# A hybrid retention and S5 layer on one core: dummy products on ones, the sample's state as moving operand, scores a slot later, a GLU operand in two pieces

## The chip, the cores and the metric

The kernel runs on one core of one Trainium2 chip. The metric is the device time of one execution in microseconds; a difference in it counts as measurable here from about 0.2% on.

## What is computed

One layer (DEPTH is 1) of a streaming encoder, for a prompt of 2048 frames and for 8 running streams of 16 frames (the sample), 1024 channels, in float32:

```python
hn = _rmsnorm(x, norm_g)
q, k, v, g_ret, u, g_ssm = split(hn @ w_in)            # 1024 x 3072
o, ret_s = _retention(rotary(q), rotary(k), v, ret_s0)  # 4 heads of 128
o = _rmsnorm(o, ret_norm_g) * silu(g_ret)
y, ssm_h = _s5(u, ssm_h0, ...)                          # 32 groups, complex scan
z = gelu(y)
z = z * sigmoid(z @ w_glu + b_glu) * silu(g_ssm)
out = x + concat([o, z]) @ w_out
y = _rmsnorm(out, final_norm_g)
```

In the retention each head keeps a state of 128x128; an output frame is its masked scores times the values plus its query times the state. For the sample there are 8 states a head, one for each stream.

## The kernel before, in words

The frames lie in 17 tiles of 128: tiles 0 to 15 are the prompt, tile 16 is the sample (8 streams of 16). Weights are split into two float16 parts, so a projection step is three products: hi by hi (L709), lo by hi (L710), hi by lo (L711) for the heads, L695 to L697 for `u` and the gate.

**The order.** The program is written out by hand in a list of slots, `stream`. A slot holds the three products of one 128-row block of the contraction (in the `u` and gate stages for one block of output columns, in the heads for one tile), and everything else hangs on a slot as a hook (`hook(i, f)` runs f right behind slot i). Each engine takes its instructions in the order of this list, and SP, which issues nearly all DMAs, too. First comes the `u` projection in six chunks of tiles, then head 0 with its 17 tiles (8 slots a tile; tile 16 is taken after tile 8), then the gate projection, heads 1 to 3 beside the S5 scans, the GLU (64 slots from `G0`), and last the output product.

**The start** (L320 to L334, L605 to L634). SP loads tile 0 and tile 1 of x, the first weights, tiles 2 to 8, then the small S5 inputs (`s5_loads`, L353 to L366), tiles 9 to 16 and the constants `C`. PE runs 13 dummy products on `warm`, a tile of zeros (L339), transposes tile 0 (`half`, L157, into the two `aux` banks and `tr`), runs 20 more dummies, and then computes the column sums of the squared weights (`mat`, L219, output `nps`), from which VectorE works out the scales of the first weights; with the transposes of tile 1 and the first split weights the stream can begin. `warm` is carved from the buffer named `ct`, and so is `hst`, into which `s5_loads` brings the S5 state of the sample.

**Weights of the next stage.** Head 0's eight weight tiles `raw` are loaded during the `u` stage by hooks from slot 9 on, every fourth slot (L183), squared on ScalarE from slot 46 on, every fifth (L196), and split later. Between these loads SP issues the stores of the finished `u` pieces (`flush_store`, L687, `ud`).

**A step of a head** (class Step; `n` is its first slot). `r0` at n+7 rotates q and k (VectorE L722, GpSimd L726) and evacuates v and the gate; `r1` at n+15 transposes q and k (L740) and copies them (`qkT`, L742); `r2` at n+17 multiplies them (`scps`, L746) and masks the scores (`sm`, L749, VectorE); `r3` at n+23 makes output and next state (L768 to L770), with `stats` for the norm (ScalarE L756, GpSimd L132 and L133, VectorE L759). `scps` lies in the bank `sc`, of which there is one and which the scale products `nps` and the third product of `sst` (below) use too.

**The sample's step** (tile 16, one a head). `r3s` at n+20 computes the output transposed: values as stationary and scores as moving operand (L787), then for each of the 8 streams its state as stationary operand and its 16 query columns as moving operand (L789); ScalarE copies the result (`oT`, L791) and at n+25 PE transposes it back (`ots`, L809). `states` at n+28 makes the new states in four banks (`sst`, L800).

**The GLU operand.** `Glu.split` scales z on ScalarE (L1275, hi part) and takes the rest on VectorE (L1276, 128x4x280), for tile t+2 while tile t is multiplied.

Of the kernel before, what the change touches and what calls it, by code (L numbers as in the profile page):

```python
# [10 lines left out]
F32 = mybir.dt.float32  # L11
# [4 lines left out]
AF = mybir.ActivationFunctionType  # L16
OP = mybir.AluOpType
# [45 lines left out]
def kernel(ctx: ExitStack, tc: tile.TileContext, eye, cst, rot, x_prompt, x_sample, state_ret,  # L63
# [5 lines left out]
    act = nc.scalar.activation  # L69
    V = nc.vector  # L70
    G = nc.gpsimd
    mm = nc.tensor.matmul
    tr = nc.tensor.transpose

    def dap(t, off, ap):
        return bass.AP(tensor=t.tensor, offset=t.offset + off, ap=ap)
# [4 lines left out]
    def right(name, st):  # L81
        return pool(name, st=st, side="right", reuse_waits="tile")
# [6 lines left out]
    def pbank(tag, name):  # L89
        return ps.tile([128, 512], F32, tag=tag, name=name, bufs=2 if tag in ("pj", "aux") else 1)  # L90
# [9 lines left out]
    ident = per.tile([128, 128], F32, name="ident")  # L100
# [12 lines left out]
    ones = per.tile([128, 128], F32, name="ones")  # L113
# [6 lines left out]
    alc, alz, syc, tsc, icc = ex[:, 16:20], ex[:, 20:21], ex[:, 21:22], ex[:, 22:23], ex[:, 23:24]  # L120
# [53 lines left out]
    class Ws:  # L174
# [10 lines left out]
        def split(self):  # L185
            d = self.t = self.dst()
            sc = self.group.gs[:, self.scale:self.scale + 1]
            act(d[:, 0, :], self.raw, AF.Copy, scale=sc)  # L188
            V.scalar_tensor_tensor(d[:, 1, :], self.raw, sc, d[:, 0, :], op0=OP.mult, op1=OP.subtract)  # L189
# [79 lines left out]
    tp = right("tp", ctx)  # L269
# [63 lines left out]
    warm = sa("ct", [128, 576])[:, 0:128]  # L333
    V.memset(warm, 0.0)  # L334
    pw = pbank("pj", "warm")

    def warm_up(n):
        for _ in range(n):
            mm(pw[:, 0:128], warm, warm, start=True, stop=True)  # L339
    warm_up(13)  # L340


    def idle(n):
# [267 lines left out]
    p = pbank("st", "smps")  # L611
# [8 lines left out]
    hns[0].half(0, "aux")  # L620
    gu.square(3, True)
    hns[0].half(1, "tr")
    warm_up(20)
    hns[1].stat()
    gu.square(4)
    gu.square(5, True)
# [72 lines left out]
    class Step:  # L699
# [37 lines left out]
        def r1(self):  # L737
# [3 lines left out]
            self.qkT = tp.tile([128, 2, 128], F32, name="qkT", bufs=2)  # L741
            act(self.qkT, p[:, 0:256].rearrange("p (q n) -> p q n", q=2), AF.Copy)  # L742

        def r2(self):
            p = pbank("sc", "scps")
            mm(p[:, 0:128], self.qkT[:, 1, :], self.qkT[:, 0, :], start=True, stop=True)  # L746
            self.sm = tp.tile([128, 128], F32, tag="sm", name="sm", bufs=1)
            L = 128 if self.t < 16 else 16
            V.scalar_tensor_tensor(self.sm, p[:, 0:128], float(GAM[self.h] ** -L), cmask if self.t < 16 else smask,  # L749
                                   op0=OP.mult, op1=OP.mult)  # L750
# [32 lines left out]
        def r3s(self):  # L783
            h_ = self.h
            Sb = self.Sb
            po = pbank("o", "ops")
            mm(po[:, 0:128], self.vt, self.sm, start=True, stop=False)  # L787
            for b in range(8):
                mm(po[:, 16 * b:16 * b + 16], Sb[:, b, :], self.qkT[:, 0, 16 * b:16 * b + 16], start=False, stop=b == 7)  # L789
            oT = tp.tile([128, 128], F32, tag="sm", name="oT", bufs=1)  # L790
            act(oT, po[:, 0:128], AF.Copy)  # L791
            self.oT = oT

        def states(self):
            Sb = self.Sb
# [7 lines left out]
                V.scalar_tensor_tensor(sv, sv, float(GAM[self.h] ** 16), pq[q].rearrange("p (b e) -> p b e", b=2),  # L803
                                       op0=OP.mult, op1=OP.add)
            dma(dap(rs_sample, self.h * 16384, [[128, 128], [65536, 8], [1, 128]]), Sb)

        def r3s2(self):
            po = pbank("tr", "ots")
            tr(po[:, 0:128], self.oT, ident)  # L809
            self.stats(po[:, 0:128])  # L810

        def r4(self):
            a = alc[:, self.h:self.h + 1]
# [9 lines left out]
    def hook(i, f):  # L823
        hooks.setdefault(max(int(i), 0), []).append(f)
# [64 lines left out]
    for s in seq:  # L889
        n = s.at  # L890
        hook(n + 7, s.r0)
        hook(n + 15, s.r1)
        hook(n + 17, s.r2)
        if s.t < 16:
            hook(n + 23, s.r3)
            hook(n + 28, s.r4)
            hook(n + 32, s.st)
        else:
            hook(n, s.r3s_load)
            hook(n + 20, s.r3s)  # L900
            hook(n + 25, s.r3s2)
            hook(n + 28, s.states)
            hook(n + 30, s.r4)
            hook(n + 33, s.st)
# [20 lines left out]
    for i in range(5):  # L925
        t, n = 4 * i, 1 if i == 4 else 4
# [5 lines left out]
    def s5(name, shape, dt=F32, bufs=1):  # L932
        return sp[0].tile(shape, dt, tag=name, name=name, bufs=bufs)
# [162 lines left out]
    for g, q in enumerate(gps):  # L1096
        n = C1 + PER * g
# [156 lines left out]
    class Glu:  # L1254
# [17 lines left out]
        def split(self):  # L1272
            z = zb[:, :, self.t, :]
            self.hl = s5("U5", [128, 4, 2, 280], F16, 2)
            act(self.hl[:, :, 0, :], z, AF.Copy, scale=syc)  # L1275
            V.scalar_tensor_tensor(self.hl[:, :, 1, :], z, syc, self.hl[:, :, 0, :], op0=OP.mult, op1=OP.subtract)  # L1276

        def mmul(self, k2):
            cb, k0 = k2 // 2, 2 * (k2 % 2)
# [28 lines left out]
    for t in range(8):  # L1308
        if t < 6:
            hook(G0 + 8 * t + 7, glus[t + 2].split)  # L1310
        n = (S5END + 3, S5END + 4, G0 + 2, G0 + 4, G0 + 22, G0 + 30, G0 + 38, G0 + 46)[t]
# [3 lines left out]
    for t in range(8):  # L1315
        for cb in range(4):
            n = G0 + 8 * t + 2 * cb + 1
# [157 lines left out]
```

## Time and profile before

| what | value |
|---|---|
| median of 3 runs | 968.43 us (967.48 to 968.7) |
| profiled execution, its own time | 965.96 us |
| its span in the trace | 964.2 us |
| VectorE, ScalarE, GpSimd busy | 66%, 45%, 35% |
| moved by DMA | 106.16 MB, mean 110 GB/s |

The span runs from the first to the last instruction of the profiled execution; its own time lies 1.8 us above. Engines are called PE (TensorE), DVE (VectorE), ACT (ScalarE), POOL (GpSimd) and SP (SyncE, the DMA issuer) in the rows; L339 is line 339 of the kernel. A product in float32 shows as two passes, so 20 products count as 40. A row of the timeline merges instructions of one line that follow each other, and the time in it runs from the first one's start to the last one's end, while products overlap: the pitch from one start to the next is shorter than the duration of one.

### The profile page before, as it was taken

What the parts mean: (1) busy time and instruction counts of PE and PEld (TensorE: products, weight loads), DVE (VectorE), ACT (ScalarE), POOL (GpSimd) and SP (SyncE); (2) the same over time, 40 slices, a digit from 0 to 9 for tenths busy, and PEclk for the clock granted to TensorE, in tenths of its full rate; (3) what the DMA queues carried; (4) which work ended last, traced back from release to release, by engine and by line L of the source; (5) the groups of instructions that cost most, each with busy time, mean ns of one, the idle gap of its engine ahead of it and who ended that gap; (6) DMA issues with size and microseconds to landing.
All of it is one profiled execution on the core that took longest, in us unless ns stands there. A gap on an engine that the chain in (4) does not pass through costs nothing.

```text
span 964.2 us, 15907 instructions
## 1 busy us (share of the span) xinstructions
PE 923.4 (96%) x5386; PEld 557.3 (58%) x5386; DVE 639.0 (66%) x1595; ACT 437.5 (45%) x1133; POOL 334.0 (35%) x620
## 2 busy tenths in 40 slices
PE   2999999999999999999999999999999999999997
PEld 2896445555687555556655566555656864444444
DVE  2569954566589756777887778887576955345344
ACT  3575323433466544545445454454434844232331
POOL 0121334432354423544565445655234420000001
PEclk7999999999999999999999999999999999999999
DMA  9696245431186435221224212374263254544542
GB/s 303 215 126 82 55 115 135 107 83 44 44 163 107 94 98 121 65 60 37 62 70 116 60 37 57 93 255 133 64 225 112 67 147 123 152 109 122 152 110 87
DMA packets 161283, 106.16 MB, mean 110 GB/s; under 512 B 80001, under 2 KB 147121, under 8 KB 160689
## 3 DMA queue, kind: packets, MB, share of 16 engines
q1 hardware_dynamic: 161056, 104.88, 42.5%
q8 instruction: 42, 0.69, 0.3%
q14 instruction: 41, 0.33, 0.1%
q10 hardware_dynamic: 144, 0.26, 0.1%
HBM read 64.69 MB, written 35.96 MB: 104 GB/s over the span
## 4 chain that ended last, share of the span: by engine, by line
PE 73%; DVE 11%; DMA 4%; ACT 4%; issue 4%; POOL 4%; SPq 0%; POOLq 0%; ACTq 0%; DVEq 0%
PE pj L709 9%; PE pj L710 9%; PE pj L711 9%; PE outps L1359 6%; PE outps L1358 6%; PE outps L1357 6%; PE ups L695 4%; PE ups L697 4%; PE ups L696 3%; PE glps L1286 2%; PE glps L1287 2%; PE glps L1288 2%; PE scps L746 1%; PE ops L770 1%; PE yps L1069 1%
## 5 line engine op out<-in xcount | busy, mean ns | idle before, releaser
L726 POOL TENSOR_TENSOR rot<-A,Pm 128x128 f32<-128x128 f32 x136 | 75.5, 574 | 120.9 <-DVE A L722 100.2
L709 PE MATMUL pj<-w,R1a 128*128 128x512 f16 x288 | 109.3, 380 | 0.0
L711 PE MATMUL pj<-w,R1a 128*128 128x512 f16 x288 | 109.1, 379 | 0.0
L710 PE MATMUL pj<-w,R1a 128*128 128x512 f16 x288 | 109.1, 379 | 0.0
L1358 PE MATMUL outps<-w,mh 128*128 128x512 f16 (+1 forms) x280 | 104.4, 373 | 0.0
L1359 PE MATMUL outps<-w,mh 128*128 128x512 f16 (+1 forms) x280 | 104.4, 373 | 0.0
L1357 PE MATMUL outps<-w,mh 128*128 128x512 f16 (+1 forms) x280 | 104.4, 373 | 0.0
L709 PE MATMUL pj<-w,R1b 128*128 128x512 f16 x256 | 97.2, 380 | 0.0
L711 PE MATMUL pj<-w,R1b 128*128 128x512 f16 x256 | 97.0, 379 | 0.0
L710 PE MATMUL pj<-w,R1b 128*128 128x512 f16 x256 | 97.0, 379 | 0.0
L729 ACT ACTIVATE vt<-pj,hv 128x128 f32<-128x128 f32 x68 | 25.0, 368 | 146.1 <-DVE A L722 144.6
L695 PE MATMUL ups<-R1a,w 128*128 128x256 f16 (+1 forms) x256 | 73.3, 286 | 2.2 <-ACT w L188 1.0
L1368 ACT ACTIVATE res<-xo 128x512 f32<-128x512 f32 (+1 forms) x35 | 21.6, 617 | 117.6 <-DVE xo L1367 69.7
L697 PE MATMUL ups<-R1a,w 128*128 128x256 f16 (+1 forms) x256 | 73.2, 286 | 0.4 <-DVE w L189 0.4
L696 PE MATMUL ups<-R1a,w 128*128 128x256 f16 (+1 forms) x256 | 73.2, 286 | 0.0
L1367 DVE SCALAR_TENSOR_TENSOR xo<-outps,ex,xo 128x512 f32<-128x512 f32 (+1 forms) x35 | 25.6, 733 | 65.2 <-PE outps L1359 65.2
L132 POOL TENSOR_TENSOR ss<-ss,C 128x1 f32<-128x1 f32 x68 | 18.8, 277 | 126.3 <-ACT sj L756 126.2
L756 ACT ACTIVATE sj<-ops 128x128 bf16<-128x128 f32 x64 | 17.7, 276 | 91.5 <-PE ops L770 91.1
L189 DVE SCALAR_TENSOR_TENSOR w<-raw,gc,w 128x512 f16<-128x512 f32 x48 | 40.8, 853 | 26.3 <-ACT w L188 26.2
L132 POOL TENSOR_TENSOR fs<-fs,half__73 128x1 f32<-128x1 f32 x16 | 3.0, 190 | 154.4 <-DVE fs L1372 154.4
L759 DVE SCALAR_TENSOR_TENSOR on<-ops,ss,gg 128x128 f32<-128x128 f32 x64 | 22.4, 350 | 47.0 <-POOL ss L133 46.7
L697 PEld LDWEIGHTS <-w 128*128 128x128 f16 x384 | 37.6, 98 | 22.1 <-DVE w L189 0.7
(352 smaller groups left out, 2373.3 us busy)
## 6 DMA issues: line engine op xcount, KB each, us to landing
raw<-in_w_in_dram SPq DMA_DIRECT2D x48, 256.0 KB
raw<-in_w_out_dram SPq DMA_DIRECT2D x32, 256.0 KB
xo<-in_x_prompt_dram SPq DMA_DIRECT2D x16, 512.0 KB
out_dram<-res SPq DMA_DIRECT2D x16, 512.0 KB
R1a<-in_x_prompt_dram SPq DMA_DIRECT2D x9, 512.0 KB
uraw<-ud SPq DMA_DIRECT2D x32, 140.5 KB
yd<-ysb SPq DMA_DIRECT2D x32, 140.0 KB
R1a<-yd SPq DMA_DIRECT2D x4, 1120.0 KB
```

The costliest lines, as they stand in the source:

```text
L189: V.scalar_tensor_tensor(d[:, 1, :], self.raw, sc, d[:, 0, :], op0=OP.mult, op1=OP.subtract)
L695: mm(ov, w[:, 0, c], hh, start=k == 0, stop=False)
L696: mm(ov, w[:, 0, c], hl, start=False, stop=False)
L697: mm(ov, w[:, 1, c], hh, start=False, stop=k == NK - 1)
L709: mm(self.pj, hh, w[:, 0, :], start=k == 0, stop=False)
L710: mm(self.pj, hh, w[:, 1, :], start=False, stop=False)
L711: mm(self.pj, hl, w[:, 0, :], start=False, stop=k == NK - 1)
L726: G.tensor_tensor(self.rot[:, :, a, :], A[:, :, a, :], Pm[:, :, 1 - a, :], OP.add if a else OP.subtract)
L1357: mm(p, m[:, k, 0, :], w[:, 0, cw], start=k == 0, stop=False)
L1358: mm(p, m[:, k, 0, :], w[:, 1, cw], start=False, stop=False)
L1359: mm(p, m[:, k, 1, :], w[:, 0, cw], start=False, stop=k == NK - 1)
L1367: V.scalar_tensor_tensor(self.x[:, c], p, icc, self.x[:, c], op0=OP.mult, op1=OP.add)
```

## The change

It does four things. The dummy products in the second batch read `ones` (L114, a tile of ones that VectorE writes at the start) instead of `warm`; the first batch is as before. In the sample's step the scores are the stationary and the values the moving operand, so the output comes out with frames on partitions; the state of a stream is now the moving operand of 128 columns and the queries are stationary, 32 columns at a time, one product for each of the four groups of 32 output partitions and for the first and second stream in it. For that `qm` holds the queries twice, with the other stream's columns zero (`r1s`: a fill on GpSimd, two copies on ScalarE, in the buffer of `Pm`). The copy `oT` and the transpose `ots` go, and `stats` follows at once; `r3s` stands at n+22 instead of n+20. `r2` stands at n+18 instead of n+17, for all tiles. `Glu.split` does its VectorE part in two pieces of 128x2x280.

```diff
--- before.py
+++ after.py
@@ -334,10 +334,10 @@
     V.memset(warm, 0.0)
     pw = pbank("pj", "warm")
 
-    def warm_up(n):
+    def warm_up(n, w):
         for _ in range(n):
-            mm(pw[:, 0:128], warm, warm, start=True, stop=True)
-    warm_up(13)
+            mm(pw[:, 0:128], w, w, start=True, stop=True)
+    warm_up(13, warm)
 
 
     def idle(n):
@@ -620,7 +620,7 @@
     hns[0].half(0, "aux")
     gu.square(3, True)
     hns[0].half(1, "tr")
-    warm_up(20)
+    warm_up(20, ones)
     hns[1].stat()
     gu.square(4)
     gu.square(5, True)
@@ -741,6 +741,13 @@
             self.qkT = tp.tile([128, 2, 128], F32, name="qkT", bufs=2)
             act(self.qkT, p[:, 0:256].rearrange("p (q n) -> p q n", q=2), AF.Copy)
 
+        def r1s(self):
+            self.qm = tp.tile([128, 2, 128], F32, tag="Pm", name="qm", bufs=1)
+            G.memset(self.qm, 0.0)
+            for a in range(2):
+                o, i = (z.rearrange("p (g b j) -> p g b j", g=4, b=2)[:, :, a, :] for z in (self.qm[:, a, :], self.qkT[:, 0, :]))
+                act(o, i, AF.Copy)
+
         def r2(self):
             p = pbank("sc", "scps")
             mm(p[:, 0:128], self.qkT[:, 1, :], self.qkT[:, 0, :], start=True, stop=True)
@@ -784,12 +791,12 @@
             h_ = self.h
             Sb = self.Sb
             po = pbank("o", "ops")
-            mm(po[:, 0:128], self.vt, self.sm, start=True, stop=False)
-            for b in range(8):
-                mm(po[:, 16 * b:16 * b + 16], Sb[:, b, :], self.qkT[:, 0, 16 * b:16 * b + 16], start=False, stop=b == 7)
-            oT = tp.tile([128, 128], F32, tag="sm", name="oT", bufs=1)
-            act(oT, po[:, 0:128], AF.Copy)
-            self.oT = oT
+            mm(po[:, 0:128], self.sm, self.vt, start=True, stop=False)
+            for b in range(2):
+                for g in range(4):
+                    r = slice(32 * g, 32 * g + 32)
+                    mm(po[r, 0:128], self.qm[:, b, r], Sb[:, 2 * g + b, :], start=False, stop=b == 1)
+            self.stats(po[:, 0:128])
 
         def states(self):
             Sb = self.Sb
@@ -803,11 +810,6 @@
                 V.scalar_tensor_tensor(sv, sv, float(GAM[self.h] ** 16), pq[q].rearrange("p (b e) -> p b e", b=2),
                                        op0=OP.mult, op1=OP.add)
             dma(dap(rs_sample, self.h * 16384, [[128, 128], [65536, 8], [1, 128]]), Sb)
-
-        def r3s2(self):
-            po = pbank("tr", "ots")
-            tr(po[:, 0:128], self.oT, ident)
-            self.stats(po[:, 0:128])
 
         def r4(self):
             a = alc[:, self.h:self.h + 1]
@@ -890,15 +892,15 @@
         n = s.at
         hook(n + 7, s.r0)
         hook(n + 15, s.r1)
-        hook(n + 17, s.r2)
+        hook(n + 18, s.r2)
         if s.t < 16:
             hook(n + 23, s.r3)
             hook(n + 28, s.r4)
             hook(n + 32, s.st)
         else:
             hook(n, s.r3s_load)
-            hook(n + 20, s.r3s)
-            hook(n + 25, s.r3s2)
+            hook(n + 16, s.r1s)
+            hook(n + 22, s.r3s)
             hook(n + 28, s.states)
             hook(n + 30, s.r4)
             hook(n + 33, s.st)
@@ -1273,7 +1275,8 @@
             z = zb[:, :, self.t, :]
             self.hl = s5("U5", [128, 4, 2, 280], F16, 2)
             act(self.hl[:, :, 0, :], z, AF.Copy, scale=syc)
-            V.scalar_tensor_tensor(self.hl[:, :, 1, :], z, syc, self.hl[:, :, 0, :], op0=OP.mult, op1=OP.subtract)
+            for c in (slice(0, 2), slice(2, 4)):
+                V.scalar_tensor_tensor(self.hl[:, c, 1, :], z[:, c], syc, self.hl[:, c, 0, :], op0=OP.mult, op1=OP.subtract)
 
         def mmul(self, k2):
             cb, k0 = k2 // 2, 2 * (k2 % 2)
```

PE at the start, before: `hnps` are the transposes of tile 0 and then tile 1, `warm` the dummies, `nps` the sums for the first scales, `ups` the `u` projection.

```order
L157 MATMUL hnps<-ident,R1a 128x128 [waits DVE_49]
L157 MATMUL hnps<-ident,R1a 128x128 x7
L339 MATMUL warm<-zf 128x128 [waits DMAHW1_49]
L339 MATMUL warm<-zf 128x128 x19
L219 MATMUL nps<-gc,ones 128x8 [waits DVE_49]
L157 MATMUL hnps<-ident,R1a 128x128 x4
L157 MATMUL hnps<-ident,R1a 128x128 [waits PE_49]
L157 MATMUL hnps<-ident,R1a 128x128 x3
```

And with the change:

```order
L157 MATMUL hnps<-ident,R1a 128x128 [waits DVE_49]
L157 MATMUL hnps<-ident,R1a 128x128 x7
L339 MATMUL warm<-ones 128x128 x20
L219 MATMUL nps<-gc,ones 128x8 [waits DVE_49]
L157 MATMUL hnps<-ident,R1a 128x128 x4
L157 MATMUL hnps<-ident,R1a 128x128 [waits PE_49]
L157 MATMUL hnps<-ident,R1a 128x128 x3
```

The dummies stand at the same place, and the wait for a DMA in front of them is gone.

PE at the sample's step of head 0, before: `ops` is the output, `Sb` the eight states.

```order
L711 LDWEIGHTS R1b
L711 MATMUL pj<-w,R1b 128x512
L787 MATMUL ops<-sm,vt 128x128 [waits DVE_49]
L789 MATMUL ops<-qkT,Sb 128x16 [waits DMAHW2_49]
L789 MATMUL ops<-qkT,Sb 128x16 x7
L709 LDWEIGHTS R1b
L709 MATMUL pj<-w,R1b 128x512
```

With the change, two slots later:

```order
L711 LDWEIGHTS R1b
L711 MATMUL pj<-w,R1b 128x512
L794 MATMUL ops<-vt,sm 128x128 [waits DVE_49]
L798 MATMUL ops<-Sb,qm 32x128 [waits DMAHW2_49,Activation_49]
L798 MATMUL ops<-Sb,qm 32x128 x3
L798 MATMUL ops<-Sb,qm 32x128 [waits Activation_49]
L798 MATMUL ops<-Sb,qm 32x128 x3
L709 LDWEIGHTS R1b
L709 MATMUL pj<-w,R1b 128x512
```

The eight narrow products become eight with 32 stationary columns; each half of them waits for ScalarE, which makes `qm`.

ScalarE around the same step, before (`oT` and `ots` belong to the sample, `qkT`, `vt` and `gg` to its neighbours):

```order
L742 ACTIVATE qkT<-qkps 128x256 [waits PE_49]
L729 ACTIVATE vt<-pj,hv 128x128 [waits DVE_49]
L735 ACTIVATE gg<-pj,gc 128x128
L815 ACTIVATE oh<-on,ex 128x128 [waits DMAHW7_49]
L791 ACTIVATE oT<-ops 128x128 [waits DVE_49,PE_49]
L188 ACTIVATE w<-raw,gc 128x512
L742 ACTIVATE qkT<-qkps 128x256 [waits PE_49,Activation_49]
L729 ACTIVATE vt<-pj,hv 128x128 [waits DVE_49,Activation_49]
L735 ACTIVATE gg<-pj,gc 128x128
L756 ACTIVATE sj,ss<-ots 128x128 [waits PE_49,Pool_49]
```

With the change:

```order
L742 ACTIVATE qkT<-qkps 128x256 [waits PE_49]
L729 ACTIVATE vt<-pj,hv 128x128 [waits DVE_49]
L735 ACTIVATE gg<-pj,gc 128x128
L749 ACTIVATE qm<-qkT 128x4x16 [waits Activation_49,Pool_49]
L749 ACTIVATE qm<-qkT 128x4x16
L817 ACTIVATE oh<-on,ex 128x128 [waits DMAHW7_49]
L188 ACTIVATE w<-raw,gc 128x512
L763 ACTIVATE sj,ss<-ops 128x128 [waits PE_49]
L742 ACTIVATE qkT<-qkps 128x256 [waits PE_49]
```

The copies of `qm` stand behind the next step's `vt` and `gg`; the copy `oT` is gone, and `sj` of the sample comes ahead of the next `qkT` instead of three rows behind it.

## Rows read from the trace of the kernel before

**Rows 1.** The page's busy times: us, share of the span, instructions.

```profile
PE 923.4 (96%) x5386; PEld 557.3 (58%) x5386; DVE 639.0 (66%) x1595; ACT 437.5 (45%) x1133; POOL 334.0 (35%) x620
```

**Rows 2.** Waits of PE over the run: us in total, times, longest.

```profile
PE warm L339 <- DMA zf<-in_state_ssm_re_dram: 14.4, 1, 14.4
...
PE scps L746 <- ACT qkT L742: 2.1, 4, 0.7
...
PE ops L770 <- DVE sm L749: 2.0, 1, 2.0
...
PE scps L746 <- DVE gc L224: 1.2, 2, 0.6
...
PE scps L746 <- DVE ex L1198: 0.8, 1, 0.8
...
PE scps L746 <- DVE woc L1170: 0.6, 1, 0.6
```

**Rows 3.** Timeline of the start: start us, us, engine, line, operation.

```profile
7.34 1.09 PE L157 MATMUL hnps<-ident,R1a 128*128 128x128 f32 x8 [1.15 <-DVE R1a L151]
...
8.66 0.69 DVE L162 TENSOR_TENSOR R1a<-hnps,R1a 128x512 f16<-128x512 f32 x1 [0.49 <-ACT R1a L161]
...
13.18 0.17 DVE L215 TENSOR_TENSOR gc<-gc,ng 128x8 f32<-128x8 f32 x1
...
22.88 7.41 PE L339 MATMUL warm<-zf 128*128 128x128 f32 x40 [14.45 <-DMA zf<-in_state_ssm_re_dram]
...
30.13 0.29 PE L219 MATMUL nps<-gc,ones 128*128 128x8 f32 x2
...
32.34 0.28 PE L695 MATMUL ups<-R1a,w 128*128 128x256 f16 x1 [1.00 <-ACT w L188]
```

**Rows 4.** Stretches of one microsecond, PE: busy, granted clock, DMA share, GB/s.

```profile
11.00:12.00 1.00, 0.00 (x0) 0.73 1.05 392
```

**Rows 5.** Stretches of two microseconds, all engines, granted clock, DMA share, GB/s.

```profile
40.00:42.00 2.00, 2.00 (x21) 1.82 (x20) 1.89 (x3) 1.09 (x2) 0.00 (x0) 1.00 0.79 263
```

**Rows 6.** Timeline of SP's queue.

```profile
46.14 3.26 SPq L687 DMA_DIRECT2D ud<-xu  x4
```

**Rows 7.** DMA view, 46 to 48 us: busy tenths in 40 slices.

```profile
DMA  0000000000900000000000000000479999999999
```

**Rows 8.** DMA view, 46 to 58 us: packets by size.

```profile
DMA packets 4781, 0.86 MB, mean 72 GB/s; under 512 B 4194, under 2 KB 4780, under 8 KB 4780
```

**Rows 9.** Timeline of ScalarE, 62 to 70 us.

```profile
64.64 0.62 ACT L196 ACTIVATE wj<-raw 128x512 bf16<-128x512 f32 x1
...
65.25 1.29 ACT L161 ACTIVATE R1a<-hnps 128x512 f16<-128x512 f32 x2
```

**Rows 10.** Timeline of PE, 66 to 72 us.

```profile
67.70 0.60 PE L157 MATMUL hnps<-ident,R1a 128*128 128x128 f32 x4
```

**Rows 11.** Timeline of PE: the sample's step of head 0; `kps` at 118 us.

```profile
221.34 1.86 PE L789 MATMUL ops<-qkT,Sb 128*128 128x16 f32 x16
223.04 0.38 PE L709 MATMUL pj<-w,R1b 128*128 128x512 f16 x1
223.26 0.38 PE L710 MATMUL pj<-w,R1b 128*128 128x512 f16 x1
...
117.93 0.64 PE L569 MATMUL kps<-zf 128*32 128x128 f32 x8 [0.17 <-DVE R1b L162]
118.50 0.39 PE L695 MATMUL ups<-R1b,w 128*128 128x512 f16 x1
```

**Rows 12.** Groups of GpSimd by line and shape: busy, mean ns.

```profile
L525 POOL MEMSET zf<- 128x1024 f32 x1 | 1.0, 951 | 9.5 <-DVE zf L492 9.5
```

**Rows 13.** Timeline of PE near 731 us.

```profile
731.25 0.49 PE L770 MATMUL ops<-vt,sm 128*128 128x128 f32 x2 [2.00 <-DVE sm L749]
```

**Rows 14.** Stretches after it, PE: busy, granted clock, DMA share, GB/s.

```profile
731.00:733.00 2.00, 1.75 (x9) 0.67 0.37 113
733.00:735.00 2.00, 2.00 (x11) 0.50 0.96 253
```

## The prediction

> **What bounds the kernel now.** I read the page's busy times first: TensorE is busy 923.4 us of 964.2 [rows 1]. With PE at 96% an engine that is less busy costs time only where PE stands still for it, so the second view was PE's waits, and every term below is a wait of PE or PE work that is dropped. One wait is in another class than all others [rows 2]: the second batch of dummy products (L339) stands 14.4 us for the load of the S5 state into `zf`. The rest are pieces of under a microsecond, but for one of 2.0 us (`ops` for `sm`).
>
> The timeline of the start [rows 3] shows what that wait holds up. The last transpose before the dummies begins at 7.34 and the eight take 1.09 us, so PE is free at 8.43. VectorE has the sums of squares ready at 13.35 (13.18 plus 0.17), and all that PE then needs for the scale product `nps` is there. But the dummies stand ahead of it in PE's order; they start at 22.88, run 7.41 us, `nps` follows at 30.13 and the first real product at 32.34. The dummies read `warm`, which is the same memory as `hst`; the load into it was issued in the program before them, so they wait for it. Meanwhile the clock is lost: granted 1.00 until about 11.5, then 0.50, that is 1.2 GHz [rows 4].
>
> **The change, part by part.**
>
> *Dummies on `ones`: 16.7 us off the start.* `ones` is written once by VectorE in the first microsecond, so the order shows no wait any more. The 20 dummies start at 8.43. Each is two passes; at 2.4 GHz the pitch is that of the transposes, (1.09 - 0.27) / 7 = 0.117 us, so 40 passes end at 8.43 + 4.7 = 13.1. `nps` is then released by VectorE at 13.35, and moves from 30.13 to 13.4: **-16.7**. The 2.2 us from `nps` to the first product stay (scales, evacuation, first split), and slot 0 begins at 15.6. The longest idle time of PE in between is the 1.0 us before the first product [rows 3], so I keep the clock at 2.4 GHz; were the dummies still at the lower level (twice the pitch), they would end at 17.8 and 4.4 of the 16.7 would be lost.
>
> *What is late next: the DMA queue, +3.0.* PE moves 16.7 us forward; the loads do not. SP's order is unchanged and its long list of small loads doesn't depend on PE. The queue empties at 41.6 (share 0.79 of 40 to 42) [rows 5]. Behind it stand the stores of `u`, issued at 46.14 [rows 6], whose first packets go at about 47.4 [rows 7]; in the change they are ready earlier and follow at once from 41.6, which is 5.8 earlier, not 16.7. Between these stores runs the load of head 0's weights, 512 packets of 512 bytes for a tile. From 46 to 58 packets of that size are 4780 - 4194 = 586 [rows 8]: tile 1 is in at 57.8. ScalarE squares it at 64.64 [rows 9], with 6.8 us to spare. In the change it lands at 57.8 - 5.8 = 52.0 and is wanted at 64.64 - 16.7 = 47.9: ScalarE stands 4.1 us. Queued behind that square on ScalarE are the two evacuations at 65.25 for tile 7; they would begin at 52.6 and the first would be done, with VectorE's part of 0.69 (L162) [rows 3], at 53.9. PE's next transposes into the same two banks start at 67.70 [rows 10], in the change at 51.0: PE waits **+2.9, taken as 3.0**. Bounds: 0, if the load comes between the stores as soon as it is issued, and 4.1, all of ScalarE's wait.
>
> *Scores a slot later: -4.5, and +1.0 back.* PE's waits ahead of `scps` add up to 2.1 + 1.2 + 0.8 + 0.6 = 4.7 us in eight places, none over 0.84 [rows 2]. A slot is three products of 0.22 us, the step from L709 to L710 [rows 11], 0.66 in all, so all but some 0.2 of the longest goes. But `scps`, the scale products `nps` and the third `sst` share the bank `sc`, and both come now two slots after a `scps` instead of three: where VectorE is late with `sm`, they wait. There are four `sst` and some six `nps`; I take a tenth of a microsecond each, 1.0 in all. Bounds: from nothing back to 4.5, the wait only moved.
>
> *Sample's state as moving operand: -3.3.* Before, 16 passes that each load a whole 128-column stationary tile of the state take 223.04 - 221.34 = 1.70 us a head, at about 0.107 each [rows 11]. Now the stationary tile is 32 columns of `qm`. The nearest row is `kps`, eight passes with 32-column weights: 0.64 long, the last 0.27, so 0.053 a pass, and 0.20 from the last to the next wide product [rows 11]. Sixteen are 15 x 0.053 + 0.20 = 1.0: 0.7 saved, and the transpose of `oT` (0.12 by the pitch above) goes too: 0.82 x 4 heads = **-3.3**. Bounds: 0 and 6.8 (the passes for nothing).
>
> `qm` adds a fill of 128x256 on GpSimd and two copies on ScalarE. GpSimd filled four times as much in 0.95 us [rows 12], and ScalarE's copy of `oT` goes. They have six slots (3.9 us) between r1s and r3s; `rot` of the next step and the fill stand before them. I cost them at nothing; without that cover it would be a microsecond a head.
>
> *GLU operand in two pieces: 0.* PE's waits name no `glps` for it; eight more fixed parts on VectorE lie beside PE.
>
> **Sum.** -16.7 + 3.0 - 4.5 + 1.0 - 3.3 = -20.5. From the profiled execution's own 965.96 that is 945.5; the runs' median lies 2.47 higher, 968.43, so the forecast is **947.9**.
>
> **A rule against the row.** The eight `kps` passes lie in two column groups, four in each, and average 0.053 all the same [rows 11]; the sum goes by that. The Trainium skill, TensorE: Matmul & The Clock Gate, section on packing small matmuls, says that products whose outputs lie in different 32-partition column groups run at the same time. By that rule four would run at once; no row here shows it for columns.
>
> **The rivals.**
> - *Four groups at once, and the loads in time.* The sixteen passes go in four rounds: 4 x 0.053 + 0.20 = 0.41, another 0.6 x 4 = 2.4 off: 945.5; with the DMA term at zero as well 942.5. For it: the groups alternate in the new order, where `kps` has four passes of one group in a row. Against: the `kps` row shows no gain from its two groups. 0.2.
> - *The waits only move.* VectorE's lateness, not the scores' place, ends `sst`, `nps` and `ops`; at 731.25 `ops` waits 2.0 us for `sm` [rows 13], and over the next two stretches of two microseconds the clock is at 0.67 and 0.50, 0.66 + 1.0 = 1.7 us lost [rows 14]. The -3.5 of the scores falls away, 951.4, and a new stall near 51 us costs one such spell, 953.1. 0.2.
> - *Slower than before.* PE without its long wait runs into the loads again and again in the `u` stage, and each time the clock falls. A microsecond at 1.2 GHz loses half of one, so the change loses when the low level lasts over 2 x 20.5 = 41 us longer than before; 60 us would give 947.9 + 30 = 977.9. Against it: one stall of 4.1 at most is left after tile 1, since the later tiles come faster than they are squared. 0.02.
>
> **How the numbers follow.** The forecast has 0.55, the rivals 0.2, 0.2 and 0.02; 0.03 is for what I don't see. The range from 942 to 953.5 takes in the first two rivals. A difference of 0.2%, 1.9 us, is about what a measurement of this kernel tells from none; all cases but the third rival and part of the unseen are far faster: 0.97, 0.01, 0.02.
>
> **What would show it.** Right: no wait at L339; `nps` at 13.4 and slot 0 at 15.6; granted clock 1.00 from 5 us on; a wait of ScalarE for `raw` near 48 us and of PE for transposes near 51; no `scps` in PE's waits; the eight state products of a head 1.0 us. Wrong: slot 0 after 18 us, a stretch of low clock in the first 100 us, or PE's waits for `sm` growing by over 3 us.

## The result, and the profile after

The changed kernel takes **955.57 us** (954.29 to 957.23) against 968.42 in the same comparison: a ratio of 0.9865, with a 95% interval from 0.9853 to 0.9878. That is 13.1 us less by the ratio, where 20.5 were forecast, and the time lies above the range's end of 953.5. The profiled execution took 956.7 us, with a span of 954.6.

PE's busy time answers to [rows 1], with 4 instructions fewer:

```profile
PE 921.2 (97%) x5382; PEld 554.2 (58%) x5382; DVE 641.7 (67%) x1603; ACT 437.9 (46%) x1137; POOL 334.1 (35%) x624
```

The timeline of PE at the start answers to [rows 3]:

```profile
7.26 1.09 PE L157 MATMUL hnps<-ident,R1a 128*128 128x128 f32 x8 [0.56 <-DVE R1a L151]
8.20 4.63 PE L339 MATMUL warm<-ones 128*128 128x128 f32 x40
14.04 0.39 PE L219 MATMUL nps<-gc,ones 128*128 128x8 f32 x2 [1.22 <-DVE gc L215]
...
16.36 0.39 PE L695 MATMUL ups<-R1a,w 128*128 128x256 f16 x1 [1.00 <-ACT w L188]
```

This part came nearly as forecast: no wait at L339, `nps` at 14.04 (13.4 was said) and the first product at 16.36 in place of 32.34, 16.0 us earlier. What became of those 16 us is in PE's waits over the run, which answer to [rows 2] (L753 is `scps`, L777 `ops`, L807 `sst`):

```profile
PE ops L777 <- DVE sm L756: 4.8, 5, 1.6
PE hnps L157 <- DVE R1a L162: 3.9, 1, 3.9
PE ups L695 <- ACT ub L673: 2.5, 1, 2.5
PE scps L753 <- ACT qkT L742: 2.5, 4, 0.8
PE yps L1071 <- ACT Vs L1027: 2.0, 1, 2.0
...
PE sst L807 <- DVE sm L756: 1.1, 1, 1.1
```

The second line is the new stall, from 50.6 us on. The row of its end, from PE's timeline:

```profile
54.50 0.90 PE L157 MATMUL hnps<-ident,R1a 128*128 128x128 f32 x3 [3.94 <-DVE R1a L162]
```

It was forecast at 2.9, with its end near 54. But what holds PE is not what I said. VectorE there, its wait for the stores first:

```profile
53.20 0.65 DVE L677 TENSOR_SCALAR xu<-ups,gc 128x256 f32<-128x256 f32 x1 [4.78 <-DMA ud<-xu]
...
53.76 0.68 DVE L162 TENSOR_TENSOR R1a<-hnps,R1a 128x512 f16<-128x512 f32 x1
...
57.76 0.69 DVE L162 TENSOR_TENSOR R1a<-hnps,R1a 128x512 f16<-128x512 f32 x1 [3.23 <-ACT R1a L161]
```

ScalarE, and SP's queue:

```profile
56.52 0.63 ACT L196 ACTIVATE wj<-raw 128x512 bf16<-128x512 f32 x1 [6.68 <-DMA raw<-in_w_in_dram]
```

```profile
37.18 10.66 SPq L687 DMA_DIRECT2D ud<-xu  x4
47.89 2.12 SPq L183 DMA_DIRECT2D raw<-in_w_in_dram  x1
```

The stores of `u` from the first evacuations had not left the buffer `xu` when VectorE wanted it again; the split (L162) that releases PE stands right behind that evacuation on VectorE. The four stores alone held SP's queue for 10.66 us, against 3.26 before [rows 6]. ScalarE's wait for the weights, which the prediction names, is there too and is longer than forecast (6.68 for 4.1). But it ends at 56.52, two microseconds after PE has started again, so it is not what PE stood for. It ends VectorE's next wait, at 57.76, and the transposes behind that one (59.25) stand for nothing.

Behind four of PE's stalls the granted clock is under 1.00 (stretches of the span: all engines' busy time, then granted clock, DMA share, GB/s); behind the one of 2.5 us that ends at 286.4 it is 1.00:

```profile
12.00:20.00 8.00, 5.60 (x37) 3.96 (x36) 6.54 (x17) 5.59 (x11) 0.51 (x2) 0.79 1.00 371
50.00:60.00 10.00, 6.06 (x32) 4.63 (x30) 3.54 (x10) 3.48 (x8) 0.65 (x2) 0.68 0.86 110
270.00:278.00 8.00, 6.17 (x40) 5.57 (x41) 3.85 (x12) 5.90 (x16) 2.29 (x5) 0.79 0.93 157
690.00:698.00 8.00, 7.21 (x31) 3.71 (x32) 4.53 (x14) 1.34 (x5) 0.74 (x2) 0.79 0.73 208
```

Each deficit times the stretch is, at most, the work lost: 0.21 x 8 = 1.7, 0.32 x 10 = 3.2 (a little of it while PE stood), 1.7 and 1.7 us. Laid product by product beside the second execution of the kernel before (e5), the changed kernel is 14.4 us ahead when it runs into the stall and 7.7 behind it: stall and low clock took 6.7.

The sample's step of head 0 answers to [rows 11]:

```profile
215.45 0.65 PE L798 MATMUL ops<-Sb,qm 128*32 128x128 f32 x16
216.02 0.39 PE L709 MATMUL pj<-w,R1b 128*128 128x512 f16 x1
```

From the first of the sixteen passes to the next wide product it is now 0.57 us, against 223.04 - 221.34 = 1.70, and the other three heads show the same to 0.01. `qm`, costed at nothing, is late by little: ScalarE's first copy waits 1.16 us for the fill, which GpSimd does behind `rot`, and begins at 214.69:

```profile
214.69 0.40 ACT L749 ACTIVATE qm<-qkT 128x64 f32<-128x64 f32 x2 [1.16 <-POOL qm L746]
```

### The profile page after: what moved, and what is told of

The parts are those of the page before. It is cut to its first block, busy times and chain, and to the rows that moved or that the text cites. A ratio compares the mean times of both kernels' runs of the same rounds, so it can differ in the third digit from the quotient of the medians.

```text
span 954.6 us, 15911 instructions
## 1 busy us (share of the span) xinstructions
PE 921.2 (97%) x5382; PEld 554.2 (58%) x5382; DVE 641.7 (67%) x1603; ACT 437.9 (46%) x1137; POOL 334.1 (35%) x624
## 4 chain that ended last, share of the span: by engine, by line
PE 77%; DVE 6%; DMA 5%; ACT 4%; issue 3%; POOL 3%; SPq 1%; POOLq 0%; ACTq 0%; DVEq 0%
PE pj L709 11%; PE pj L710 11%; PE pj L711 11%; PE outps L1360 6%; PE outps L1362 6%; PE outps L1361 6%; PE ups L695 3%; PE ups L697 3%; PE ups L696 3%; DMA raw<-in_w_in_dram 2%; PE ops L777 2%; PE glps L1289 2%; PE glps L1291 2%; PE glps L1290 2%; PE scps L753 1%
## 5 line engine op out<-in xcount | busy, mean ns | idle before, releaser
L695 PE MATMUL ups<-R1a,w 128*128 128x256 f16 (+1 forms) x256 | 75.1, 293 | 3.7 <-ACT ub L673 2.5
L697 PE MATMUL ups<-R1a,w 128*128 128x256 f16 (+1 forms) x256 | 74.7, 292 | 0.2 <-DVE w L189 0.2
L696 PE MATMUL ups<-R1a,w 128*128 128x256 f16 (+1 forms) x256 | 74.8, 292 | 0.0
L763 ACT ACTIVATE sj<-ops 128x128 bf16<-128x128 f32 x68 | 18.8, 276 | 94.5 <-PE ops L777 92.6
```

The source lines that it names most:

```text
L695: mm(ov, w[:, 0, c], hh, start=k == 0, stop=False)
L696: mm(ov, w[:, 0, c], hl, start=False, stop=False)
L697: mm(ov, w[:, 1, c], hh, start=False, stop=k == NK - 1)
```

## The experiments

Each kernel was timed beside the kernel before on the same chip; e5 is a single execution. "By ratio" is (1 - ratio) x 968.4. The kernel before took 969.46 us beside e1 to e4, 968.72 beside e5 to e8, 969.16 beside e9 to e12 and 968.29 beside e13 and e14, so between these groups the ratio says more than the median. F is the changed kernel with the scores back at slot 17.

| kernel | median us | ratio, 95% interval | by ratio |
|---|---|---|---|
| changed kernel | 955.57 | 0.9865 [0.9853, 0.9878] | -13.1 |
| e1: before + dummies on ones | 961.48 | 0.9908 [0.9891, 0.9924] | -8.9 |
| e2: before + sample's step | 962.28 | 0.9917 [0.9903, 0.9931] | -8.0 |
| e3: before + scores a slot later | 969.24 | 0.9992 [0.9982, 1.0001] | -0.8 |
| e4: F | 953.32 | 0.9828 [0.9814, 0.9843] | -16.7 |
| e5: before once more | 968.12 | - | - |
| e6: F + four x tiles loaded later | 948.34 | 0.9796 [0.9776, 0.9817] | -19.8 |
| e7: F + weights ahead of the stores of u | 957.63 | 0.9879 [0.9857, 0.9902] | -11.7 |
| e8: F + squares later in the gate stage | 956.40 | 0.9869 [0.9846, 0.9891] | -12.7 |
| e9: e6 + weights later in the gate stage | 945.08 | 0.9749 [0.9729, 0.9768] | -24.3 |
| e10: e6 + eight more dummies | 951.97 | 0.9806 [0.9784, 0.9829] | -18.8 |
| e11: e6 + transposes of q, k at slot 14 | 957.30 | 0.9870 [0.9850, 0.9890] | -12.6 |
| e12: e6 + GLU operand in one piece | 948.64 | 0.9782 [0.9763, 0.9802] | -21.1 |
| e13: before + ones + four x tiles later | 956.98 | 0.9882 [0.9863, 0.9901] | -11.4 |
| e14: e9 + two more x tiles later | 943.98 | 0.9748 [0.9726, 0.9769] | -24.4 |

### The parts, one by one

**e1.** Of the diff only the lines on `warm_up` (the second batch multiplies `ones`).

> The kernel before with only the dummies on ones. By the prediction's sum -16.7 + 3.0 = -13.7 us. Theory DMA (what I now think): the first product moves 16 us forward, but the loads for slots behind it don't; PE then stands about 4 us for the second half of a tile near 54 us and runs some 7 us at the lower clock behind it, so about -8 us at 75 us already here; if the second loss, that of the gate stage (4 to 5 us near 270 to 290 us in the changed kernel), also comes from the earlier start, then -3 to -5 us at the end. Rival: the scores' later slot makes the gate-stage loss; then it is absent here and -8 to -9 us stays at the end.

Measured -8.9. The stall is there without any other part of the change, and its longest wait has the same 3.9 us (PE's waits, 40 to 70 us):

```profile
PE hnps L157 <- DVE R1a L162: 4.7, 2, 3.9
```

So the dummies alone fall 4.8 short of the sum's -13.7. Product by product beside e5, this kernel is 15.6 us ahead at the first product, 14.0 when it meets the stall and 7.2 behind it: the stall and the low clock took 6.8, where the sum has 3.0. Where PE stands in the gate stage is taken up with e5.

**e2.** Of the diff only `r1s`, the new `r3s`, its two hooks and the lost `r3s2`.

> The kernel before with only the sample's state as moving operand in four column groups. By the prediction's sum -3.3 us (0.82 a head). By the rule that four groups run at once -5.7 us (1.4 a head). By the changed kernel's own steps, which gained 1.7 a head, -6.9 us, with the gain of one head visible as a shorter pitch of the eight products L798.

Measured -8.0 by ratio and -7.2 by the medians, more than any of the three. The passes give (1.70 - 0.57) x 4 = 4.5 and the transposes that are gone 0.12 x 4 = 0.5. Product by product beside e5, the gain at the four steps is 1.4, 1.3, 1.3 and 1.2 us, 5.2 in all, so this is the size of the term; the same steps gain as much between e1 and e4. Behind the step of head 0 another 0.8 goes (`sst`, which waited 0.9 us for `sm` before, does not wait here), over the gate stage 1.4, and at the start 0.8 is lost, as the wait at L339 is 16.0 us here and 15.0 in e5. That makes the 6.6 between the two executions. The gate stage differs by more than 1.4 between two executions of one kernel (e5), so that part is not shown to come from the change; what else is in the -8.0 stays open.

**e3.**
```diff
-        hook(n + 17, s.r2)
+        hook(n + 18, s.r2)
```

> The kernel before with only the scores a slot later. By the prediction's sum -3.5 us (-4.5 off scps, +1.0 on nps and sst). Rival, the waits only move: 0 within 1.5 us; PE's waits before scps fall by 3 to 4 us and those of ops for sm grow by as much. Third: slower by 1 to 3 us, as the later sm makes on, oh and the store of oh later, and SP stands longer for oh with the loads behind it.

Measured -0.8, with an interval that holds 0: the second theory. PE's waits of this kernel (L746 is `scps`, L770 `ops`, L800 `sst`):

```profile
PE ops L770 <- DVE sm L749: 4.3, 5, 1.9
PE sst L800 <- DVE sm L749: 2.2, 2, 1.2
...
PE scps L746 <- ACT qkT L742: 2.1, 3, 0.8
```

`ops` grew from 2.0 to 4.3 and `sst` from 0.9 to 2.2, and the wait for `qkT` stayed at 2.1 [rows 2]; all waits of `scps` fell from 4.7 to 2.3.

**e4.** The reverse edit in the changed kernel.

> The changed kernel with the scores back at slot 17. If the waits only moved: the same as the changed kernel within 1.5 us (about 955.6), with waits before scps back near 8 and ops for sm down by 4. If the later slot makes the gate-stage loss (stalls near 272 and 286 us): 3 to 5 us faster, about 951 to 952, and no low clock near 272 us. By the prediction 3.5 us slower.

Measured 953.32, a ratio of 0.9828 against 0.9865, and the intervals do not meet: in the changed kernel the later slot costs about 3.6 us by ratio, 2.3 by the medians. `ops` waits 1.9 for `sm` in place of 4.8. The same four stretches as above, in this kernel:

```profile
12.00:20.00 8.00, 5.18 (x45) 4.19 (x44) 6.77 (x19) 5.43 (x11) 0.63 (x1) 1.00 0.99 373
50.00:60.00 10.00, 5.54 (x27) 4.41 (x28) 3.86 (x12) 3.84 (x9) 0.17 (x1) 0.66 0.93 127
270.00:278.00 8.00, 7.28 (x63) 6.63 (x64) 4.22 (x9) 6.10 (x18) 2.32 (x5) 1.00 0.94 188
690.00:698.00 8.00, 7.18 (x39) 3.88 (x38) 5.87 (x28) 2.16 (x7) 1.63 (x4) 1.00 0.93 268
```

Of four spells of low clock only the one behind the stall at 54 us is left. The spell near 16 us cannot come from the scores, which begin far later, so an execution has it or not; that the one near 272 hangs on them is not shown. Nor does the loss lie in the gate stage alone: of the 3.9 us between the two executions 1.3 are there by the end of head 0, 2.6 by the end of the gate stage, and the rest comes after. Stalls of about the same length, 1.8 us here and 2.0 there, both for `Vs` near 271 us, were followed by a fall in one execution and by none in the other.

**e5.** The kernel before, unchanged.

> The kernel before once more, for a second profiled execution. In all four experiments and in the changed kernel PE waits 1.8 to 2.4 us for ACT's Vs near 270 to 282 us, in the profiled execution of before only 1.0. If that execution was a favourable one: here the wait at yps is near 2 us as well, PE loses 2 to 4 us between 265 and 300 us against it, and the time is 968 to 970. Rival: the changes make that loss; then here the wait is again 1.0 and the first products after 300 us start within 1 us of the first execution.

It took 968.12 us, and the loss is there. PE's waits between 262 and 302 us:

```profile
PE ups L695 <- ACT ub L673: 3.9, 2, 2.2
PE yps L1069 <- ACT Vs L1025: 1.7, 1, 1.7
```

In the first profiled execution of before the same two were 0.4 and 0.9. So the waits of the gate stage, which look like new ones when the changed kernel is laid beside that execution, belong to the kernel before too; its profile, 2.47 us under its median, was one that met them at their smallest.

### What holds PE near 54 us

**e6.** On F:
```diff
-    for t in range(9, 17):
+    for t in range(9, 13):
         hns[t].load()
...
+    for t in range(13, 17):
+        hook(30 + 4 * (t - 13), hns[t].load)
```

> The changed kernel with scores at slot 17, and the loads of x tiles 13 to 16 issued at slots 30 to 42, behind the first stores of u and most loads of head 0's weights. Theory queue: the stores of u and the weights are late because 4 MB of x stand ahead of them; with 2 MB less ahead the stall of 4.7 us near 54 us and the low clock behind it go: 5 to 7 us less than with scores at 17 alone, about 947. Rival, the stores are slow in themselves (packets of 132 bytes): the stall stays at 3 us or more, 951 to 954. Slower, if tile 13 (wanted near 56 us) now comes late: a wait of ACT for R1b.

Measured 948.34, 5.0 under e4 by the medians and 3.1 by ratio, where the intervals just touch (0.9814 and 0.9817); in the traces the gap grows by 4.8 us at the stall. That is the queue. VectorE's wait for the stores is gone, and PE's for the split is down from 4.7 to 1.7 (VectorE 30 to 70 us, then PE 40 to 70):

```profile
DVE xu L677 <- DMA ud<-xu: 0.2, 1, 0.2
```

```profile
PE hnps L157 <- DVE R1a L162: 1.7, 2, 0.9
```

ScalarE still waits 4.2 us for the weights there, in two pieces; the first of PE's two waits, 0.9 us at 53.58, stands behind it.

**e7.** On F, for the group of head 0 (`i == 1`):
```diff
-            hook(ld + (4 if i == 1 else 5) * k, grp.ws[k].load)
+            hook(3 + k if i == 1 else ld + 5 * k, grp.ws[k].load)
```

> The changed kernel with scores at slot 17, and head 0's eight weight loads issued at slots 3 to 10, ahead of the first stores of u. By the prediction's step (ACT's square waits for the weights, the evacuations behind it) the stall near 54 us goes: 946 to 948. Rival, VectorE's evacuation into xu waits for the stores of u, and the split behind it on VectorE: those stores are now later by up to 8 weight loads (11 us), and the stall grows to 6 us or more: 954 to 960.

Measured 957.63, 4.3 over e4. ScalarE's wait for the weights is gone from its list, and PE's stall has grown all the same, as VectorE's for the stores did (VectorE 30 to 70 us, then PE 40 to 70):

```profile
DVE xu L677 <- DMA ud<-xu: 9.0, 1, 9.0
```

```profile
PE hnps L157 <- DVE R1a L162: 8.2, 1, 8.2
```

e6 and e7 together settle what holds PE in the changed kernel: removing the prediction's cause made the stall longer, and taking traffic from ahead of the stores shortened it to pieces under a microsecond. The weights are the next in line, as e10 shows.

**e13.** e1 with the edit of e6.

> The kernel before with only the dummies on ones, and the loads of x tiles 13 to 16 issued at slots 30 to 42. The dummies alone gave -8.6 (ratio 0.9908), 4.8 less than the prediction's -13.7. If the loads ahead of the stores of u are the whole of what is missing: 4 to 6 us below the dummies alone, a ratio of 0.985 to 0.987, and the first products after 75 us 12 to 14 us ahead of before. Rival: the gain of the later loads seen in e6 depends on the other parts of the change: 0 to 2 us below the dummies alone.

Measured 0.9882, 2.5 under e1 by ratio and 4.5 by the medians, between the two theories, and the intervals touch (0.9901 and 0.9891). PE's wait for the split is 2.5 us here, against 4.7 in e1. In the traces the products behind 75 us are 12.1 us ahead of e5, where e1 has 7.2. So the loads are most of what was missing there; by ratio they are about half of it, and they are not shown to be all.

**e10.** On e6, `warm_up(23, ones)` for 20, and `warm_up(5, ones)` ahead of the first slot.

> The kernel of e6, with three more dummies ahead of the scale product and five more ahead of slot 0, in PE's idle stretches of 0.7 and 1.2 us. Theory: these idle stretches let the clock fall near 16 us for 3.4 us, which costs 1.7 us of work; filled, the granted clock stays 1.00 and the time falls by 1 to 2 us, 946.5 to 947.5. Rival: the clock falls from what lies earlier, or the dummies delay slot 0 by as much as they save: 948 to 949.

Measured 951.97: 3.6 over e6 by the medians, but 1.0 by ratio, with intervals that lie over each other, and the five runs fall into two groups (948.4 and 949.0; 952.0 to 952.8). So it is not shown to be slower than e6; faster, as the theory said, it is not. The profiled execution is the slowest of the five. The clock was kept at the start, and lost later (all engines at 16 to 18 and at 54 to 58 us):

```profile
16.00:18.00 2.00, 1.60 (x15) 1.25 (x15) 1.91 (x6) 1.98 (x4) 0.00 (x0) 1.00 1.01 395
...
54.00:56.00 2.00, 0.17 (x2) 0.17 (x2) 0.91 (x3) 2.00 (x6) 0.00 (x0) 1.00 1.00 131
56.00:58.00 2.00, 2.00 (x12) 1.65 (x12) 1.65 (x6) 2.00 (x6) 0.19 (x1) 0.57 1.06 178
```

In e6 the clock was 0.50 at 16 to 18 and 1.00 at 54 to 58. The start is not faster: the first product comes at 17.09 us, in e6 at 15.87, and in front of the stall the two are within 0.1 us of each other, so the dummies delay slot 0 by as much as they save. And the stall that came back is the prediction's own chain. VectorE waits only 0.7 us for the stores, but ScalarE stands for the weights of head 0, VectorE for ScalarE and PE for VectorE:

```profile
53.85 0.63 ACT L196 ACTIVATE wj<-raw 128x512 bf16<-128x512 f32 x1 [4.35 <-DMA raw<-in_w_in_dram]
```

```profile
55.09 0.69 DVE L162 TENSOR_TENSOR R1a<-hnps,R1a 128x512 f16<-128x512 f32 x1 [4.92 <-ACT R1a L161]
```

```profile
55.83 0.74 PE L157 MATMUL hnps<-ident,R1a 128*128 128x128 f32 x4 [3.07 <-DVE R1a L162]
```

Once the stores are out of the way, the weights hold PE. Why they landed 2.2 us later than in e6 is open. The gate stage adds to this execution: one wait of 2.4 us, and a granted clock of 0.66 from 280 to 290 us.

### The gate stage, the transposes, the GLU

**e8.** On F, for the weights of head 1 (`i == 3`), which are loaded in the gate stage (`ld`, `sq`, `sc` and `sp_` are the slots of their loads, squares, scale and splits; only the added lines are shown, here and in e9):
```diff
+        if i == 3:
+            sq, sc, sp_ = f0 + 44, f0 + 96, [f0 + 108 + 7 * k for k in range(8)]
```

> The changed kernel with scores at slot 17; the squares of head 1's weights, that fall in the gate stage, stand 24 slots later (and the scale and the splits behind them). Theory: ACT's Vs and ub stand behind squares that wait for weights just loaded; the waits of PE near 271 and 283 us (2.0 and 1.1 us) go to under 0.7: 2 to 3 us less, about 950.5 to 951.5. Rival: Vs waits for its own chain (v, U, uraw): no change within 1 us.

Measured 956.40, 3.1 over e4: a miss. `Vs` was in time, and the wait came back larger one step on (255 to 300 us):

```profile
PE ups L695 <- ACT ub L673: 6.6, 2, 6.3
```

ScalarE stood 5.2 us there for `wv`, whose load had been issued at 274.46 and was used at 282.50: late squares did not help. That the loads themselves stood ahead is the reading that e9 tests.

**e9.** On e6:
```diff
+        if i == 3:
+            ld, sq, sc, sp_ = f0 + 96, f0 + 112, f0 + 156, [f0 + 164 + 3 * k for k in range(8)]
```

> The kernel of e6 (948.3), with head 1's weights loaded at slots 96 to 131 of the gate stage, squared at 112 to 147, scaled at 156 and split from 164 on (before: loads from slot 8, squares from 20). Theory: between 264 and 280 us the DMA queues are at 0.9 with g's stores in packets of 132 bytes, and these 2 MB stand ahead of the loads of u and of v's weights; with them behind 300 us the waits of PE between 260 and 300 us (1.3, 1.6, 1.6, 1.4) fall to under 1.5 in all: 3 to 4 us less, 944 to 946. Rival: the stores of g alone fill the queues: the waits stay at 4 us or more, 947 to 949.

Measured 945.08, 3.3 under e6 by the medians and 4.6 by ratio, and the intervals do not meet: the loads of the weights stood ahead. PE's waits between 250 and 302 us are small ones now, led by

```profile
PE scps L753 <- ACT qkT L742: 0.7, 1, 0.7
PE ups L695 <- ACT ub L673: 0.5, 1, 0.5
```

**e14.** e9 with `range(9, 11)`, and tiles 11 to 16 at `18 + 4 * (t - 11)`.

> The kernel of e9 (945.1), with the loads of x tiles 11 and 12 moved behind slot 18 as well (11 to 16 at slots 18 to 38). Theory: the 0.9 us left before transposes near 60 us and 0 to 3 us near 54 (it came back in two kernels whose start was faster) go with 1 MB less ahead of the stores of u: 1 to 2 us less, 943 to 944. Rival: tile 11 now comes late, ACT waits for R1b and the stall returns near 47 us: 945 to 949.

Measured 943.98, not told from e9, as the intervals nearly coincide. Between 40 and 70 us PE's waits hold no `hnps` any more, only 0.2 us before `ups`.

**e11.** On e6, `hook(n + 14, s.r1)` for `n + 15`.

> The kernel of e6, with the transposes of q and k a slot earlier (14), scores at 17: two slots more or less than the product has now between them and the scores, without a later sm. Theory: the 3.0 us in five waits of scps for qkT and most of the small ones go, and nothing moves behind them: 3 to 5 us less, 943.5 to 945.5. Rival: the transposes now wait for rot: qkps enters PE's waits with as much, 947.5 to 949.5.

Measured 957.30, 9.0 over e6 by the medians and 7.2 by ratio: the rival, and worse. PE waits now ahead of the transposes:

```profile
PE qkps L740 <- POOL rot L726: 3.0, 5, 1.8
...
PE qkps L740 <- DVE Sb L810: 1.6, 2, 0.8
```

**e12.** On e6, the one `scalar_tensor_tensor` of before in `Glu.split`.

> The kernel of e6, with the GLU operand's second part in one piece again, as before the change. By the prediction 0: the same within 0.7 us, and no product of the GLU in PE's waits in either. Rival: the halves let the first products start earlier, and one piece costs 0.5 us at each of the eight steps, 951 to 952.

Measured 0.3 us above e6 by the medians and 1.3 under it by ratio, and the intervals lie over each other: no effect that this resolves, as forecast.

## Why the prediction was wrong

By its own terms, with the runs of the parts alone:

| term | forecast | measured |
|---|---|---|
| dummies on ones, with the DMA behind them | -16.7 + 3.0 = -13.7 | -8.9 (e1) |
| scores a slot later | -4.5 + 1.0 = -3.5 | -0.8 alone (e3), about +3.6 in the whole (e4) |
| sample's state | -3.3 | -8.0 (e2), of it 5.2 at the four steps |
| GLU in two pieces | 0 | not told from 0 (e12) |

**The dummies** were right: the wait at L339 went and the first product came 16.0 us earlier, where 16.7 were forecast. **The step that failed first is "what is late next: the DMA queue, +3.0".** Place and moment were right (a stall of PE that ends near 54 us), by luck: the chain that gave them is not the one that held PE, and the price was wrong. I followed the weights into ScalarE and took the stores of `u` to "follow at once" when the queue empties. But it was `xu`, the buffer of those stores, that VectorE waited for (e6, e7); the chain through ScalarE comes second, and holds PE only where the stores are in time (e10). I had read how long the stores were issued [rows 6] and not who waits to write over their source. And I priced the standing alone: 2.9 forecast, 3.9 measured. The granted clock of 0.68 over the ten microseconds from 50 us cost up to 3.2 more; together 6.7, as the products show. I had the rows for this [rows 13, 14] and used them in a rival only; the stall should have carried it in the sum. The clock at the start, which I expected to keep, fell too: 1.7 us between 12 and 20 us, in that execution. Of the signs that the prediction named for being wrong, low clock in the first 100 us came, and PE's waits for `sm` (`ops` and `sst`) grew by 3.0, from 2.9 to 5.9, just at the mark.

**The scores: the second rival, "the waits only move".** The sum counted what went from `scps` and a tenth of a microsecond for each product behind it. e3 shows 2.3 more at `ops` and 1.3 more at `sst`: VectorE's `sm` is the late one, and moving the product that feeds it gives nothing. The sum has no term for `ops`, though its one wait for `sm` was the largest left in [rows 2]; only the rival named it. Why the later slot costs more in the whole (e4) than alone (e3) is open.

**The sample's step: the size of the term.** I took 0.053 from `kps` as the price of one pass by itself. It is half the price of a pair: `kps` already gains from its two column groups. In the kernel before (stretches with these passes alone; the first x counts those that have begun, as none ends before 118.20):

```profile
117.90:118.00 0.10, 0.07 (x2) 0.10 (x4) 1.00 0.02 5
118.00:118.10 0.10, 0.10 (x4) 0.10 (x6) 1.00 0.00 0
```

Two begin in each tenth of a microsecond. With four groups, in the changed kernel, four begin together, and none in the time between (none ends before 215.74):

```profile
215.44:215.47 0.03, 0.02 (x4) 0.03 (x4) 1.00 0.00 0
215.47:215.57 0.10, 0.10 (x4) 0.10 (x8) 1.00 0.00 0
215.57:215.61 0.04, 0.04 (x8) 0.04 (x8) 1.00 0.00 0
215.61:215.68 0.07, 0.07 (x8) 0.07 (x4) 1.00 0.00 0
215.68:215.72 0.04, 0.04 (x12) 0.04 (x8) 1.00 0.00 0
```

So the rounds begin 0.11 to 0.13 us apart, about what a single pass took before (0.107 in the sample's step, 0.117 in the transposes). The rows don't name the group of a pass; that a round has as many passes as there are groups is what ties the two. The prediction's own numbers had this: 0.053 is half of 0.107, the gain that it says the row does not show, and its first rival priced a round of four at 0.053 for the same reason. With 0.107 a round, 3 x 0.107 + 0.20 = 0.52 us a head and 0.12 for the transpose give (1.70 - 0.52 + 0.12) x 4 = 5.2, and 5.2 was measured at the steps. The Trainium skill (TensorE: Matmul & The Clock Gate, the section on packing small matmuls) says that such products run at the same time, and the trace agrees with it.

**Of the rivals** "four groups at once, and the loads in time" had its first half right in kind, with a round too cheap, and its second wrong; "the waits only move" was right on the scores and too low by 2.5 us at its upper end. By the kernels with one part, two errors of opposite sign, 4.7 at the sample's step and 4.8 at the dummies, nearly cancel, which is luck; what leaves the forecast 7.4 short is about the size of the scores' error, 3.5 + 3.6. The dummies and the sample's step add up (-8.9 - 8.0 = -16.9, against -16.7 in e4, which has both and the GLU in two pieces); it is the scores that don't.

## What to carry to other kernels

A price per pass that is half of what a pass takes by itself says that two run at once; divide before you call it the price of one. When a long wait at the head of the program goes, every transfer behind it keeps its clock: list for each buffer that is stored who writes it next, not only who reads what is loaded, and price the low clock behind the stall with the stall. A load that is wanted late and issued early is paid by whoever comes after it in the queue; moving four tiles' loads and one group's weights to later slots gave 7.6 us by ratio (e4 to e9). And one profiled execution is not the kernel: a second one of before showed that a loss which seemed new was old.

## What the runs showed of the hardware

Stores in small packets held the issuing queue itself when loads stood ahead of them: four stores took 10.66 us of SP's queue, where the same four took 3.26 [rows 6]. While they drain, little moves for the share that is busy:

```profile
50.00:52.00 2.00, 0.56 (x6) 0.25 (x3) 0.00 (x0) 0.00 (x0) 0.65 (x2) 1.00 0.73 34
```

34 GB/s at a share of 0.73, against 371 at 1.00 between 12 and 20 us, where whole rows of x are loaded. The Trainium skill, DMA: Bandwidth & Descriptors, its specifications, puts the smallest transfer at line rate at 512 bytes. The stores' runs here are 33 columns of 4 bytes, 132, and 222 of the 302 packets of that stretch are under 512 bytes; the trace agrees, and shows no size between.

Float32 products into different column groups ran together: two at a time in `kps`, four at a time in the sample's step, the rounds 0.11 to 0.13 us apart. And the clock near 16 us, with PE idle for 1.2 and 1.0 us ahead of it, fell in the changed kernel (0.79 over eight microseconds) and not in e4 (1.00), whose start is the same code and where PE was idle for 1.4 and 1.0.
